# A hybrid encoder layer on one core: a fourth pair of k-tiles as seven products, and work moved between VectorE and ScalarE

## The chip, the cores and the metric

The kernel runs on one core of one Trainium2 chip. The core has five engines that each run their own list of instructions in order and wait for each other by semaphores: TensorE (PE: matrix products; PEld is its loading of the stationary operand), VectorE (DVE), ScalarE (ACT), GpSimd (POOL) and SyncE (SP), which issues most of the DMAs. The metric is the time of one execution in microseconds. The kernel before takes 1113.62 us, the median of three runs from 1113.46 to 1114.1.

## The reference

The layer maps x (256 tokens x 2048, float32) through a norm, one wide input projection, two groups of heads, an output projection and a gate. Cut to what matters:

```python
proj = rmsnorm(x, norm_w) @ w_in            # 2048 x 9*2048
q, v, f_fwd, f_bwd, z_a, b_gate, c_gate, h_b, z_b = split(proj)
# group A, 16 heads of 128, forward and backward:
f = lb + (1 - lb) * sigmoid(f_logit); k = 1 - f
o_a = chunked_linear_recurrence(silu(q), k, v, log(f))       # chunks of 64
o_a = head_rmsnorm(o_a) * silu(z_a)
# group B, 16 groups of 128:
o_b = rmsnorm(b_gate * conv3(c_gate * h_b)) * silu(z_b)
h = x + concat(o_a, o_b) @ w_out
h = h + (p @ w_ple) * sigmoid(h @ w_ple_gate)
out = rmsnorm(h, final_norm_w)
```

## The kernel before

**Products.** Every float32 operand is split into a high and a low part (fp32r), and a product is the sum of high by high, high by low and low by high. The weights come from DRAM through `Stream` (`ws`): a DMA on SP into one of three `raw` tiles, then by halves ("parts") a cast on ScalarE (L121) and a subtraction on VectorE (L122) into one of five `spl` tiles. `get` splits three parts ahead of the part that is used.

**Input projections.** `gemm_in` computes two heads' columns in 16 k-tiles. A k-tile has four products: for each of two accumulators a long one of 512 columns (L428) and a short one of 256 (L426), in the order of `PLAIN`, or of another table where `orders` names one for that k-tile: ONE turns k-tile 1, BOTH turns 1 and 5, TURNED turns 1. `tick()` behind each k-tile counts time in the program, and `at(dt, fn)` puts a function dt ticks later. The order on each engine is that of the framework's scheduler, which looks at priorities and its own estimate of when things are ready; `keep_in_program_order` pins an instruction.

**Group A.** `two_pairs(i)` for i = 0, 2, 4, 6 runs two stages (i, e), e = 0 and 1. A stage has the three projections FF, FB and Q (forget gates forward and backward, and q), each evacuated by a copy of `r` on ScalarE (L488) and an addition on VectorE (L489). `mix_forgets` then makes log f (L624, ScalarE) and 1-f (L628, VectorE), `mix_pair` the scans, exponentials and, on POOL, `kc`, `qc` and `kx`; `scores` the products L736, the masked copies L784 and the product `cx` (L780); `outputs` the product `o` (L799), its squares (L803, ScalarE) and its copy to `ogz` (L804, VectorE). `rest` is issued behind the next pair's first stage: `finish_two` takes the root of the squares' sums (L643, ScalarE) and multiplies `ogz` by root and gate (L649, VectorE), `turn` transposes the result on PE (L659), 32 ticks on, where Q of the next pair's second stage begins: in (2,1), (4,1) and (6,1).

**v and z_a.** For i = 0 they are two separate products (`gemm_two`); for i = 2, 4, 6 `gemm_vz(i)` (here vz2, vz4, vz6) takes both at once, as eight pairs of k-tiles. A pair is 24 products of 512 columns, or, for the pairs in `VZ_SUMS`, seven blocks of three, which is 21 (`half`, L548 to L550), with sums of x (`xsums`, made once, on VectorE at L533, L536 and L544) and sums of weight blocks. The weight sums of a pair in `VZ_OWN` are added on VectorE from the loaded tiles (L83). Those of another pair are prepared in a DRAM tile: `prepare` copies four blocks there from SP (L330), `add_up` adds others in three steps by POOL's accumulating DMAs, and `get` loads them as any weight. Before, VZ_OWN holds all the pairs of VZ_SUMS, and the tiles in DRAM serve the output projection only.

**Order of the stages.** Three first projections fed by DMA (manual order), (0,1), `gemm_two` for V and ZA, then (2,0), (2,1), vz2, (4,0), (4,1), vz4, (6,0), (6,1), vz6; group B with 32 projections of the same form; the output projection; gate and p; the tail.

Of the kernel before, what the change touches and what calls it, by code (L numbers as in the profile page):

```python
# [17 lines left out]
P = 128  # L18
# [119 lines left out]
def tile_hymba_encoder(  # L138
# [26 lines left out]
    xp = xctx.enter_context(tc.tile_pool(name="xp", bufs=1, side="left"))  # L165
# [5 lines left out]
    ws = Stream(tc, rawp, splp, 3)  # L171


    VZ_ORDER, VZ_SUMS, VZ_OWN = range(8), (2, 4, 6), (2, 4, 6)
    dramp = ctx.enter_context(tc.tile_pool(name="dramp", bufs=1, space=bass.MemoryType.DRAM))
    vz_prepared = {}
    blocks = {}
# [57 lines left out]
    rx, rb, rf, most, dummy = (few[:, 2 * j : 2 * j + 2] for j in range(5))  # L235
# [21 lines left out]
    cvw, th = vec[:, 3:6, :], vec[:, 6:10, :].rearrange("p (d j) c -> p d j c", d=2)  # L257


    wz = const.tile([P, P], F32, name="wz")  # L260
    dve.memset(wz, 0.0)

    act.activation(dummy[:, 0:1], wz[:, 0:1], AF.Copy)
# [6 lines left out]
    ident = const.tile([P, P], F32, name="ident")  # L270
# [1 line left out]
    ones = const.tile([P, 1], F32, name="ones")  # L272
    pool.memset(ones, 1.0)

    early = const.tile([P, 2048], F32, name="early")
    smask = early[:, 0:T]
    pool.memset(smask, 1.0)
    pool.memset(smask.rearrange("p (c t) -> p c t", t=CH)[:, :, 0:1], 0.0)
# [3 lines left out]
    for j in range(4):  # L282
        sgn = 1 if j < 2 else -1
        pool.affine_select(
            out=tri[:, j, :], in_=tri[:, j, :], compare_op=ALU.is_ge, fill=0.0, base=0,
# [9 lines left out]
        dve.memset(t, 0.0)  # L295


    mx = const.tile([P, 2, 16], F32, name="mx")
    et = const.tile([P, 2, 2, 16], F32, name="et")
    esum = const.tile([P, 2, 16], F32, name="esum")  # L300
    lb = const.tile([P, 2, 16], F32, name="lb")
    oml = const.tile([P, 2, 16], F32, name="oml")
    noml = const.tile([P, 2, 16], F32, name="noml")
# [60 lines left out]
    xs = xsp.tile([P, NKT, 2, T], F32R, name="xs")  # L364
# [8 lines left out]
    rbc = const.tile([P, T], F32, name="rbc")  # L373
    rbc2 = early[:, T : 2 * T]
    ss8 = const.tile([P, 2, 4], F32, name="ss8")
    rw = [const.tile([P, P], F32, name=f"rw{m}") for m in range(2)]

    def load_tokens(m):
        nc.sync.dma_start(xf32[:, 8 * m : 8 * m + 8].rearrange("p k t -> p (k t)"), xtok[:, m])
# [12 lines left out]
    def x_norms():  # L392
        dve.tensor_reduce(out=rx, in_=ss8, op=ALU.add, axis=AX.X)
        act.activation(rx, rx, AF.Sqrt, bias=epst, scale=1.0 / D)
        dve.reciprocal(out=rx, in_=rx)
        for m in range(2):
            dve.tensor_copy(rw[m], rx[:, m : m + 1].broadcast_to([P, P]))

    def norms_spread():
        rps = psm.tile([P, 512], F32, tag="y", name="rps")  # L400
        for m in range(2):
            pe.matmul(rps[:, m * P : (m + 1) * P], lhsT=rw[m], rhs=ident, start=True, stop=True)
        dve.tensor_copy(rbc, rps[:, :T])  # L403
        dve.tensor_tensor(out=rbc2, in0=rbc, in1=rbc, op=ALU.mult)

# [8 lines left out]
    ONE = {1: SHORTS}  # L414
# [112 lines left out]
    at(14, norms_spread)  # L527


    def act_sums(src, a, s):  # L530


        dve.tensor_tensor(out=a, in0=src[:, :, 0], in1=src[:, :, 1], op=ALU.add)  # L533
        a11, a21, a12, a22 = (a[:, k, m * P : (m + 1) * P] for k in range(2) for m in range(2))
        for o, x, y in ((0, a21, a22), (1, a21, a11), (2, a11, s[:, 0]), (3, a12, s[:, 2])):
            dve.tensor_tensor(out=s[:, o], in0=x, in1=y, op=ALU.subtract)  # L536
# [74 lines left out]
    def mix_forgets(i, xf, qt):  # L611

        by_norms(xf.rearrange("p a b t -> p (a b) t"), rbc, 4)
        by_norms(qt, rbc, 2)
        act.activation(xf, xf, AF.Sigmoid)
        sg = ap_.tile([P, 2, T], F32, tag="sg", name=f"sq{i}")
        act.activation(sg, qt, AF.Sigmoid)
        pool.tensor_tensor(out=qt, in0=qt, in1=sg, op=ALU.mult)

        lf = ap_.tile([P, 2, 2, T], F32, tag="lf", name=f"lf{i}")  # L620
        for d in range(2):
            for h in range(2):
                hd = 2 * i + h
                act.activation(  # L624
                    lf[:, d, h, :], xf[:, d, h, :], AF.Ln,
                    bias=lb[:, d, hd : hd + 1], scale=oml[:, d, hd : hd + 1],
                )
                dve.tensor_scalar(  # L628
                    xf[:, d, h, :], xf[:, d, h, :], noml[:, d, hd : hd + 1], oml[:, d, hd : hd + 1],
                    op0=ALU.mult, op1=ALU.add,  # L630
                )
        return lf

# [34 lines left out]
    def mix_pair(i, xf, qt, lf, here=False):  # L668
# [121 lines left out]
        def outputs(vt, ogz, ss):  # L790

            s, sx = st
            o = psm.tile([P, 2, 2, P], F32, tag="y", name=f"o{i}")
            for h in range(2):
                c = (2 * (i % 2) + h) * P
                hs = slice(c, c + P)
                for m in range(2):
                    pe.matmul(o[:, m, h, :], lhsT=s[:, h, m, :], rhs=vt[:, m, hs], start=True, stop=False)
                    pe.matmul(o[:, m, h, :], lhsT=sx[:, h, 1 - m, :], rhs=vt[:, 1 - m, hs], start=False, stop=True)  # L799
            junk = ap_.tile([P, P], F32, tag="jk", name=f"jk{i}")  # L800
            for h in range(2):
                for m in range(2):
                    act.activation(junk, o[:, m, h, :], AF.Square, accum_out=ss[:, m, h : h + 1])  # L803
            dve.tensor_copy(ogz, o)  # L804

        return scores, outputs

# [5 lines left out]
    def two_pairs(i):  # L813
# [18 lines left out]
        if i == 2:  # L832

            def xsums(z):
                k = 2 * VZ_SUMS[z]
                a, t = xq[1][:, 0].rearrange("p (k t) -> p k t", k=2), xq[1][:, 1].rearrange("p (o t) -> p o t", o=4)
                act_sums(xs[:, k : k + 2], a, t)
                act_split(xq[0][:, z], xs[:, k : k + 2], t)

            for z in range(len(VZ_SUMS)):  # L840
                at(10 + 12 * z, lambda z=z: xsums(z))
        for e in range(2):
            xf = ap_.tile([P, 2, 2, T], F32, tag="xf", name=f"xf{i + e}", bufs=2)
            qt = ap_.tile([P, 2, T], F32, tag="qt", name=f"qt{i + e}")
            first3 = i + e == 0

            kicks = {(0, 1): ({}, ONE, BOTH), (2, 0): (ONE, BOTH, {}), (2, 1): ({}, {}, {})}
            kicks |= {(4, 0): (ONE, TURNED, BOTH), (6, 0): (ONE, TURNED, BOTH)}
            kick = kicks.get((i, e), ({}, {}, BOTH if i + e else {}))
            for j, (c, dst) in enumerate(((B_FF, xf[:, 0]), (B_FB, xf[:, 1]), (B_Q, qt))):  # L850

                acc, offset = acc3[j] if first3 else gemm_in(c, i + e, kick[j]), 500 if e and j == 2 else 200
                evac(acc, lambda m, dst=dst: dst[:, m, :], ap_, offset)

            def mix(e=e, xf=xf, qt=qt):
# [413 lines left out]
```

## Time and profile before

| | |
|---|---|
| median of 3 runs | 1113.62 us |
| profiled execution | 1113.2 us, of it span 1111.2 us |
| around the span | 2.0 us |
| mean granted TensorE clock | 0.998 |
| stages on PE, starts | V and ZA end at 128.2; (2,1) 161.5; vz2 195.7; (4,0) 239.6; (4,1) 278.9; vz4 313.2; (6,0) 357.1; (6,1) 396.4; vz6 430.7; group B 474.6 to 835.6 us |

How to read it: a row of the timeline has start, duration, engine, line, operation and tiles (out <- in), and in brackets how long the engine stood idle before and for whom. Matrix products overlap, so the distance of two starts is what one costs, not its duration. A group has count, busy time and mean duration in ns. A window lists the busy time of PE, PEld, DVE, ACT and POOL in a stretch.

### The profile page before, as it was taken

To read this page: it belongs to the slowest core of one execution; us is meant where nothing else is said; L and a number is where in the kernel's file an instruction comes from. 1 tells how busy PE (TensorE), PEld (TensorE's weight loads), DVE (VectorE), ACT (ScalarE), POOL (GpSimd) and SP (SyncE) were. 2 spreads that over 40 slices of the span, in tenths; PEclk is the share of its full clock that TensorE was granted. 3 is DMA by queue.
4 is the path that set the end of the run, shared out by engine and by line. 5 is a ranking of instruction groups with operands and counts; after the bars stand their busy time and mean duration, and the time that the engine had idled before them with its cause. 6 is when DMAs were issued, how large, how long until landed. Compare 5 with 4: busy or idle time off the path is not lost.

```text
span 1111.2 us, 16886 instructions
## 1 busy us (share of the span) xinstructions
PE 1100.2 (99%) x6455; PEld 947.7 (85%) x6455; DVE 854.4 (77%) x1127; ACT 675.4 (61%) x946; POOL 267.1 (24%) x215
## 2 busy tenths in 40 slices
PE   9999999999999999999999999999999999999997
PEld 8888888888888888888888888888888888888886
DVE  7899468996889778998657848856767888877673
ACT  7787567767876697675535534534546575575562
POOL 1035116103430325043333223424331000000101
PEclk9999999999999999999999999999999999999999
DMA  9755555474447844658999998999979987887542
GB/s 349 271 166 172 183 190 169 135 265 152 159 147 263 305 152 152 224 171 234 299 305 262 255 340 222 289 328 264 290 202 297 326 297 286 288 312 251 196 133 76
DMA packets 69808, 260.44 MB, mean 234 GB/s; under 512 B 7008, under 2 KB 16608, under 8 KB 52192
## 3 DMA queue, kind: packets, MB, share of 16 engines
q1 hardware_dynamic: 60480, 242.25, 62.1%
q0 software_dynamic: 8960, 16.78, 9.8%
q8 instruction: 51, 0.84, 0.3%
q10 hardware_dynamic: 288, 0.34, 0.1%
q14 instruction: 29, 0.24, 0.1%
HBM read 257.25 MB, written 35.65 MB: 264 GB/s over the span
## 4 chain that ended last, share of the span: by engine, by line
PE 93%; DVE 3%; POOL 1%; issue 1%; ACT 1%; DMA 0%; DVEq 0%; ACTq 0%
PE a L428 36%; PE a L426 18%; PE avz L548 3%; PE avz L549 3%; PE avz L550 3%; PE pg L1030 3%; PE pg L1031 3%; PE pg L1029 3%; PE pa L548 2%; PE pa L550 2%; PE pa L549 2%; DVE spl L122 1%; PE pb_sc L550 1%; PE pb_sc L548 1%; PE pb_sc L549 1%; PE cx L780 1%
## 5 line engine op out<-in xcount | busy, mean ns | idle before, releaser
L122 DVE TENSOR_TENSOR spl<-raw,spl 128x1024 fp32r<-128x1024 f32 (+2 forms) x419 | 505.1, 1222 | 165.4 <-ACT spl L121 158.2
L428 PE MATMUL a<-xs,spl 128*128 128x512 f32 x1792 | 621.9, 393 | 0.6 <-DVE xs L368 0.6
L121 ACT CAST spl<-raw 128x1024 fp32r<-128x1024 f32 (+2 forms) x419 | 413.0, 999 | 250.3 <-PE a L426 96.4
L426 PE MATMUL a<-xs,spl 128*128 128x256 f32 x1792 | 494.8, 279 | 0.0
L428 PEld LDWEIGHTS a<-xs,spl 128*128 128x128 f32 x1792 | 334.0, 187 | 74.0 <-ACT spl L121 0.7
L426 PEld LDWEIGHTS a<-xs,spl 128*128 128x128 f32 x1792 | 337.1, 189 | 2.9 <-DVE spl L122 0.3
L1146 POOL TENSOR_TENSOR hh<-hh,fw 128x512 f32<-128x512 f32 (+1 forms) x9 | 10.9, 1225 | 250.7 <-ACT gt L1145 248.0
L488 ACT COPY r<-a 128x256 f32<-128x256 f32 x112 | 40.4, 368 | 34.6 <-PE a L426 33.0
L548 PE MATMUL avz<-spl,xs 128*128 128x512 f32 x138 | 54.0, 391 | 0.0
L550 PE MATMUL avz<-spl,xs 128*128 128x512 f32 x138 | 53.7, 389 | 0.0
L549 PE MATMUL avz<-spl,xs 128*128 128x512 f32 x138 | 53.7, 389 | 0.0
L717 POOL TENSOR_TENSOR qc<-pf,ge 128x256 f32<-128x256 f32 x16 | 22.0, 1379 | 106.7 <-ACT dd L707 89.1
L1029 PE MATMUL pg<-spl,ht 128*128 128x512 f32 (+1 forms) x120 | 45.2, 377 | 0.0
L1030 PE MATMUL pg<-spl,ht 128*128 128x512 f32 (+1 forms) x120 | 45.0, 375 | 0.0
L1031 PE MATMUL pg<-spl,ht 128*128 128x512 f32 (+1 forms) x120 | 45.0, 375 | 0.0
L493 POOL TENSOR_TENSOR xf<-xf,rbc 128x1024 f32<-128x1024 f32 x8 | 20.8, 2603 | 96.9 <-DVE rbc L403 49.5
L121 ACT CAST spl<-early 128x1024 fp32r<-128x1024 f32 (+1 forms) x29 | 28.7, 990 | 19.6 <-PE pb_y L550 7.5
L122 DVE TENSOR_TENSOR spl<-early,spl 128x1024 fp32r<-128x1024 f32 (+1 forms) x29 | 32.8, 1147 | 8.3 <-ACT spl L121 7.8
L548 PE MATMUL pa<-spl,mixa 128*128 128x512 f32 x88 | 34.5, 392 | 0.0
L550 PE MATMUL pa<-spl,mixa 128*128 128x512 f32 x88 | 34.3, 390 | 0.0
L549 PE MATMUL pa<-spl,mixa 128*128 128x512 f32 x88 | 34.3, 389 | 0.0
L946 POOL TENSOR_TENSOR cg<-cg,hb 128x512 f32<-128x512 f32 x8 | 13.7, 1718 | 79.2 <-DVE hb L489 79.2
(321 smaller groups left out, 1650.5 us busy)
## 6 DMA issues: line engine op xcount, KB each, us to landing
raw<-in_w_in_dram SPq DMA_DIRECT2D x106, 1024.0 KB, 7.0
raw<-in_w_in_dram SPq DMA_DIRECT2D x100, 256.0 KB, 3.9
raw<-in_w_out_dram SPq DMA_DIRECT2D x36, 512.0 KB, 5.6
sums<-in_w_out_dram SPq DMA_DIRECT2D x32, 512.0 KB, 10.4
raw<-in_w_in_dram SPq DMA_DIRECT2D x26, 512.0 KB, 5.5
raw<-sums SPq DMA_DIRECT2D x13, 1024.0 KB, 5.2
raw<-in_w_gate_dram SPq DMA_DIRECT2D x9, 1024.0 KB, 4.9
sums<-in_w_out_dram POOLq DMA_DIRECT2D x16, 512.0 KB, 10.5
```

Of the source, the lines that this page charges most:

```text
L121: self.nc.scalar.copy(out=v[:, :, 0], in_=r)
L122: self.nc.vector.tensor_tensor(out=v[:, :, 1], in0=r, in1=v[:, :, 0], op=ALU.subtract)
L426: pe.matmul(a[:, :T], lhsT=lhsT, rhs=xs[:, kt, 0, :], start=False, stop=(kt == NKT - 1))
L428: pe.matmul(a, lhsT=lhsT, rhs=xs[:, kt, :, :].rearrange("p s n -> p (s n)"), start=(kt == 0), stop=False)
L488: act.copy(out=r, in_=acc[m][:, 1, :])
L548: pe.matmul(acc, lhsT=ah, rhs=w[:, 0], start=start, stop=False)
L549: pe.matmul(acc, lhsT=ah, rhs=w[:, 1], start=False, stop=False)
L550: pe.matmul(acc, lhsT=al, rhs=w[:, 0], start=False, stop=stop)
L717: pool.tensor_tensor(out=c64(dst[:, d]), in0=c64(src[:, d, :, half * P : (half + 1) * P]), in1=g.unsqueeze(3).broadcast_to([P, 2, 2, CH]), ...
L1029: pe.matmul(acc[m], lhsT=lh, rhs=wh, start=(kt == 0), stop=False)
L1030: pe.matmul(acc[m], lhsT=lh, rhs=wl, start=False, stop=False)
L1031: pe.matmul(acc[m], lhsT=ll, rhs=wh, start=False, stop=(kt == nk - 1))
```

## The change

A pair more is taken as seven products, pair 5, with its weight sums in DRAM. 1-f goes from VectorE to an Identity activation on ScalarE (32 instructions), and the copy of `o` to `ogz` goes from VectorE to ScalarE (8). The first addition of each of x's sums is pinned to its place in the program. Three tables of product orders change. Some small tiles move to other pools, so that the larger `xsum` fits.

```diff
-    VZ_ORDER, VZ_SUMS, VZ_OWN = range(8), (2, 4, 6), (2, 4, 6)
+    VZ_ORDER, VZ_SUMS, VZ_OWN = range(8), (2, 4, 5, 6), (2, 4, 6)
...
-    rw = [const.tile([P, P], F32, name=f"rw{m}") for m in range(2)]
...
+        rw.append(ap_.tile([P, 2, P], F32, tag="s", name="rw"))
...
-    def act_sums(src, a, s):
-        dve.tensor_tensor(out=a, in0=src[:, :, 0], in1=src[:, :, 1], op=ALU.add)
+    def act_sums(src, a, s, place=lambda instr: instr):
+        place(dve.tensor_tensor(out=a, in0=src[:, :, 0], in1=src[:, :, 1], op=ALU.add))
...
-                dve.tensor_scalar(
-                    xf[:, d, h, :], xf[:, d, h, :], noml[:, d, hd : hd + 1], oml[:, d, hd : hd + 1],
-                    op0=ALU.mult, op1=ALU.add,
+                act.activation(
+                    xf[:, d, h, :], xf[:, d, h, :], AF.Identity,
+                    bias=oml[:, d, hd : hd + 1], scale=noml[:, d, hd : hd + 1],
                 )
...
-            dve.tensor_copy(ogz, o)
+            act.copy(out=ogz, in_=o)
...
-                act_sums(xs[:, k : k + 2], a, t)
+                act_sums(xs[:, k : k + 2], a, t, tc.keep_in_program_order)
...
-            kicks = {(0, 1): ({}, ONE, BOTH), (2, 0): (ONE, BOTH, {}), (2, 1): ({}, {}, {})}
-            kicks |= {(4, 0): (ONE, TURNED, BOTH), (6, 0): (ONE, TURNED, BOTH)}
+            kicks = {(0, 1): ({}, {k: SHORTS for k in (1, 5, 9)}, BOTH), (2, 0): (ONE, BOTH, {}), (2, 1): ({}, {}, {})}
+            kicks |= {(i, e): ((ONE, TURNED, BOTH), ({}, {}, {}))[e] for i in (4, 6) for e in range(2)}
```

`kick.get` gave Q of (4,1) and (6,1) the table BOTH before; now it is empty. From L400 on the new code's lines stand two further down (L643 is now L645, L659 is L661).

The scheduler orders the engines anew. **ScalarE in (4,1)**, from the last square (L803) of the pair before on, as it was:

```order
L803 ACTIVATE jk_2714,ss_1332<-o_2705 128x128
L121 CAST spl_2811<-raw_2809 128x4x256
L488 COPY r<-a_4_1_2631 128x256
L706 ACT_TABLE_LOAD
L706 ACTIVATE pf_2755<-dd_2756 128x512
L643 ACT_TABLE_LOAD
L643 ACTIVATE ss_1332<-ss_1332,epst 128x8
L121 CAST spl_2830<-raw_2809 128x4x256
```

The root of `ss` stood one cast (L121) behind the last square. Now, on the same engine and in the same stage, the stretch that ends with it (`spl_2932`, `spl_2961` and `spl_2982` are the first three parts of Q's weights, `a_5_0` FF's and FB's accumulators):

```order
L121 CAST spl_2932<-raw_2930 128x4x256
L490 COPY r<-a_5_0_2816 128x256
L490 COPY r<-a_5_1_2817 128x256
L121 CAST spl_2961<-raw_2930 128x4x256
L709 ACT_TABLE_LOAD
L709 ACTIVATE dd_2784<-dd_2784 128x512
L121 CAST spl_2982<-raw_2980 128x4x256
L645 ACT_TABLE_LOAD
L645 ACTIVATE ss_1341<-ss_1341,epst 128x8
L121 CAST spl_3027<-raw_2980 128x4x256
```

The root now stands six casts behind the last square. From the first of the four squares to it stand on ScalarE, apart from seven casts, one L630, a load and an activation for `ge`, two evacuation copies, two `pf`, two `dd`, the copy of `ogz`, and the gates `sq` and two `sz` with their loads.

**PE where Q of (4,1) begins**, before and now (`ogt` are the transposes of the two heads' `ogz`, `a_5_0` and `a_5_1` the accumulators of Q):

```order
L659 MATMUL ogt_2968<-ident,ogz_2447 128x128 x4
L659 MATMUL ogt_2977<-ident,ogz_2704 128x128 x4
L428 MATMUL a_5_0_2992<-xs,spl_2899 128x512
L426 MATMUL a_5_0_2992<-xs,spl_2899 128x256
L428 MATMUL a_5_1_2993<-xs,spl_2899 128x512
```

```order
L661 MATMUL ogt_3001<-ident,ogz_2474 128x128 x4
L661 MATMUL ogt_3010<-ident,ogz_2732 128x128
L430 MATMUL a_5_0_3025<-xs,spl_2932 128x512
L428 MATMUL a_5_0_3025<-xs,spl_2932 128x256
L430 MATMUL a_5_1_3026<-xs,spl_2932 128x512
L661 MATMUL ogt_3010<-ident,ogz_2732 128x128 x3
L428 MATMUL a_5_1_3026<-xs,spl_2932 128x256
```

Three of Q's products stand between the fifth transpose and the last three. On VectorE, the order behind the new root is the reciprocal, four L651, the split of `spl_3027`, two L651, the first half of FB's evacuation, two L651. (6,1) has the same orders on all three engines.

**VectorE ahead of the second scores of the pair i = 0** (L784, in the new code L786, behind the gate logarithms), before and now, from the end of Q's evacuation in (0,1) on:

```order
L489 TENSOR_TENSOR qt_518<-a_1_1_783,r 128x256
L122 TENSOR_TENSOR spl_907<-raw_904,spl_907 128x2x512
L708 TENSOR_TENSOR dd_654<-xf_497,dd_654 128x512
L122 TENSOR_TENSOR spl_922<-raw_904,spl_922 128x2x512
L628 TENSOR_SCALAR xf_517<-xf_517,noml,oml 128x256 x2
L122 TENSOR_TENSOR spl_940<-raw_937,spl_940 128x2x512
L628 TENSOR_SCALAR xf_517<-xf_517,noml,oml 128x256
L122 TENSOR_TENSOR spl_955<-raw_937,spl_955 128x2x512
L628 TENSOR_SCALAR xf_517<-xf_517,noml,oml 128x256
L544 TENSOR_TENSOR xsum<-xd,xsum 128x4x128
L122 TENSOR_TENSOR spl_1056<-raw_1053,spl_1056 128x2x512
L784 COPY_PREDICATED early<-early,scps_164 128x512
```

```order
L491 TENSOR_TENSOR qt_518<-a_1_1_784,r 128x256
L122 TENSOR_TENSOR spl_912<-raw_909,spl_912 128x2x512
L122 TENSOR_TENSOR spl_927<-raw_909,spl_927 128x2x512
L122 TENSOR_TENSOR spl_945<-raw_942,spl_945 128x2x512
L122 TENSOR_TENSOR spl_960<-raw_942,spl_960 128x2x512
L122 TENSOR_TENSOR spl_1061<-raw_1058,spl_1061 128x2x512
L786 COPY_PREDICATED early<-early,scps_166 128x512
```

The instructions of 1-f have left VectorE. x's sums, of which three stood before these copies (three L533, twelve L536, three L544), now all stand in (2,0), behind both masked copies of this pair.

More of the change, by code (lines that the diff above doesn't have):

```diff
@@ L257, in tile_hymba_encoder @@
     cvw, th = vec[:, 3:6, :], vec[:, 6:10, :].rearrange("p (d j) c -> p d j c", d=2)
-    wz = const.tile([P, P], F32, name="wz")
+    early = const.tile([P, 2048], F32, name="early")
+    wz = early[:, 1024 : 1024 + P]
     dve.memset(wz, 0.0)
@@ L273, in tile_hymba_encoder @@
     pool.memset(ones, 1.0)
-    early = const.tile([P, 2048], F32, name="early")
     smask = early[:, 0:T]
@@ L295, in tile_hymba_encoder @@
         dve.memset(t, 0.0)
-    mx = const.tile([P, 2, 16], F32, name="mx")
-    et = const.tile([P, 2, 2, 16], F32, name="et")
-    esum = const.tile([P, 2, 16], F32, name="esum")
+    mx = xp.tile([P, 2, 16], F32, name="mx")
+    et = xp.tile([P, 2, 2, 16], F32, name="et")
+    esum = xp.tile([P, 2, 16], F32, name="esum")
     lb = const.tile([P, 2, 16], F32, name="lb")
@@ L395, in x_norms @@
         dve.reciprocal(out=rx, in_=rx)
+        rw.append(ap_.tile([P, 2, P], F32, tag="s", name="rw"))
         for m in range(2):
-            dve.tensor_copy(rw[m], rx[:, m : m + 1].broadcast_to([P, P]))
+            dve.tensor_copy(rw[0][:, m], rx[:, m : m + 1].broadcast_to([P, P]))
+    rw = []
     def norms_spread():
@@ L401, in norms_spread @@
         for m in range(2):
-            pe.matmul(rps[:, m * P : (m + 1) * P], lhsT=rw[m], rhs=ident, start=True, stop=True)
+            pe.matmul(rps[:, m * P : (m + 1) * P], lhsT=rw[0][:, m], rhs=ident, start=True, stop=True)
         dve.tensor_copy(rbc, rps[:, :T])
```

## The prediction

> **What bounds the kernel now.** I read the page's totals and slices first, then the chain, then the list of what TensorE (PE) waited for.
>
> ```profile
> span 1111.2 us, 16886 instructions
> ...
> PE 1100.2 (99%) x6455; PEld 947.7 (85%) x6455; DVE 854.4 (77%) x1127; ACT 675.4 (61%) x946; POOL 267.1 (24%) x215
> ...
> PEclk9999999999999999999999999999999999999999
> ...
> PE 93%; DVE 3%; POOL 1%; issue 1%; ACT 1%; DMA 0%; DVEq 0%; ACTq 0%
> ```
>
> ```profile
> engine line waited for: us in total, times, longest us
> PE wps L266 <- DVE wz L261: 1.1, 1, 1.1
> PE cx L780 <- POOL kx L723: 1.1, 1, 1.1
> PE a L428 <- DVE xs L368: 0.6, 1, 0.6
> ```
>
> PE is busy for 99% of the span, at full clock in every slice, and the chain runs through it. It has one wait in the body, 1.1 us before `cx`. So the time moves in three ways only: columns that PE no longer streams, the pace at which products follow each other, and new holes in PE's stream. I price these three against the profiled run: its span of 1111.2 us and 2.0 us around it are 1113.2 us, 0.4 under the median of 1113.62. About 0.2%, or 2.23 us, is what a measurement of this kernel can tell from no change.
>
> **The products.** Three `gemm_vz` calls each turn a pair of 24 products into one of 21, so nine products of 512 columns go.
>
> ```profile
> 201.01 0.39 PE L549 MATMUL avz<-spl,xs 128*128 128x512 f32 x1
> ...
> 205.79 0.39 PE L549 MATMUL avz<-spl,xs 128*128 128x512 f32 x1
> ```
>
> The 21 steps between these two starts take 4.78 us, 0.2276 each (the 0.39 us of a row overlap the next). Nine are **-2.05 us**, and PE has nothing to put in their place.
>
> **The wait before cx.** The chain behind the one body wait runs through a DVE that is full: 49.30 of 50 us in the window that precedes it.
>
> ```profile
> core 0: us, PE busy (x) PEld busy (x) DVE busy (x) ACT busy (x) POOL busy (x), PEclk, DMA share, GB/s
> ...
> 50.00:100.00 50.00, 50.00 (x333) 42.52 (x333) 49.30 (x71) 38.26 (x51) 19.46 (x13) 1.00 0.52 169
> ```
>
> ```profile
> 94.19 1.37 DVE L784 COPY_PREDICATED early<-early,scps 128x512 f32<-128x512 uint32 x2
> ...
> 104.10 0.68 DVE L708 TENSOR_TENSOR dd<-xf,dd 128x512 f32<-128x512 f32 x1
> ```
>
> ```profile
> 103.05 3.35 POOL L717 TENSOR_TENSOR kc<-dd,ge 128x256 f32<-128x256 f32 x1 [6.22 <-DVE pf L709]
> ...
> 111.16 1.91 POOL L723 TENSOR_TENSOR kx<-kc,ge 128x512 f32<-128x512 f32 x1
> ```
>
> DVE reaches the masked copies L784 at 94.19, then the scans and L708/L709; POOL starts at 103.05 and hands over `kx` at 113.07. The change takes out of DVE's order ahead of L784 the eight L628, and of the three early sums three L533, twelve L536 and three L544, as the third pair of lists above shows.
>
> ```profile
> L628 DVE TENSOR_SCALAR xf<-xf,noml,oml 128x256 f32<-128x256 f32 x32 | 13.9, 442 | 4.6 <-ACT lf L624 4.6
> ...
> L536 DVE TENSOR_TENSOR xd<-xd 128x128 f32<-128x128 f32 x12 | 4.0, 370 | 0.2
> ...
> L533 DVE TENSOR_TENSOR xd<-xs 128x512 f32<-128x512 f32 x3 | 2.1, 688 | 0.1
> ...
> L544 DVE TENSOR_TENSOR xsum<-xd,xsum 128x512 fp32r<-128x512 f32 x3 | 2.0, 681 | 0.0
> ```
>
> That is 8 x 0.44 + 2.1 + 4.0 + 2.0 = 11.6 us of work. A tenth of it moving the chain is enough, and the tick that issues the scores is late next. I take the whole wait: **-1.1 us**. The bound on the other side is 0, if `kx` stays where it is.
>
> The four sums now stand in the stage (2,0). Their 4 x 2.7 us (11.6 - 3.5 us is three of them) and one more split lie there on a DVE with room: 30.20 us busy in 100 to 150 us by the same table of windows, with PE working on products that need only the splits. I cost them at nothing; without that cover they would hold a split back by about one sum, 2.7 us.
>
> ```profile
> 100.00:150.00 50.00, 48.94 (x340) 42.27 (x339) 30.20 (x32) 28.61 (x48) 11.36 (x7) 1.00 0.56 190
> ```
>
> **Other product orders.** In-projections run at two paces. A long and a short product in a fast one take 11.09 us for 32 pairs, as FF of (4,1) does from 278.85 to 289.94; a slow one takes about 0.2 us more.
>
> ```profile
> 278.85 0.39 PE L428 MATMUL a<-xs,spl 128*128 128x512 f32 x1
> ...
> 289.94 0.39 PE L428 MATMUL a<-xs,spl 128*128 128x512 f32 x1
> ...
> 301.04 1.03 PE L659 MATMUL ogt<-ident,ogz 128*128 128x128 f32 x8
> 301.83 0.48 PE L428 MATMUL a<-xs,spl 128*128 128x512 f32 x1
> ...
> 313.18 0.40 PE L548 MATMUL avz<-spl,xs 128*128 128x512 f32 x1
> ```
>
> ```profile
> 184.49 0.48 PE L428 MATMUL a<-xs,spl 128*128 128x512 f32 x1
> ...
> 195.68 0.39 PE L548 MATMUL avz<-spl,xs 128*128 128x512 f32 x1
> ```
>
> Q of (4,1), after its eight transposes and with BOTH, takes 313.18 - 301.83 = 11.35 us. Q of (2,1), after the same transposes with no turned order, takes 11.19. The change takes BOTH from Q of (4,1) and (6,1): 2 x -0.16 = **-0.3 us**. FB of (0,1) gets three turned k-tiles for one. Slow with one, it may stay so (0) or turn fast (-0.2, with its Q -0.4); its nearest row is its own, so 0.
>
> **The seven-product pair itself.** Pair 5 now brings seven blocks of 512 to split where a plain pair has four, in 21 steps of 0.2276 = 4.78 us. Then pair 6 has its own sums added on DVE.
>
> ```profile
> L83 DVE TENSOR_TENSOR raw<-raw 128x1024 f32<-128x1024 f32 x9 | 14.3, 1588 | 0.0
> ...
> L83 DVE TENSOR_TENSOR raw<-raw 128x512 f32<-128x512 f32 x18 | 13.7, 762 | 0.6
> ```
>
> DVE needs 3.5 x 1.13 us for pair 5's splits and 1.59 + 2 x 0.76 = 3.1 us for the sums: 7.1 us against 9.56 us of PE in the two pairs, plus pair 6's own 3.5 x 1.13 = 4.0. That is 11.1 us: DVE falls 1.5 us behind, and `Stream` splits three parts ahead, two to three of 1.13 us at that point, 2.3 to 3.4 us. I take 0.1 us for each call, **+0.3 us**, between 0 and 0.9 (the shortfall, if the lead is half gone). The sums in DRAM come by POOL's queue in three steps; the page has these transfers for w_out:
>
> ```profile
> sums<-in_w_out_dram POOLq DMA_DIRECT2D x16, 512.0 KB, 10.5
> ```
>
> POOL has 11.36 us of work in the whole of 100 to 150 us. Three steps of 10.5 us from 114 us, when `kx` and its followers are out, are done by 146; vz2 starts at 195.68 and asks later still. Hidden; late, they would cost up to a transfer of 10.5 us a call.
>
> **The head norm before the turn.** The cost that I find is on ScalarE. The 1-f of eight instructions a pair and two copies of `ogz` now stand in its order ahead of the square root `ss`, and the order shown above for (4,1) has that root after the cast of the third Q part, where before it stood one cast behind the squares.
>
> ```profile
> 277.65 0.28 ACT L803 ACTIVATE jk<-o 128x128 f32<-128x128 f32 x1 [0.88 <-PE o L799]
> ...
> 282.66 1.28 ACT L643 ACT_TABLE_LOAD   x1
> 283.95 0.30 ACT L643 ACTIVATE ss<-ss,epst 128x8 f32<-128x8 f32 x1
> 284.16 1.04 ACT L121 CAST spl<-raw 128x1024 fp32r<-128x1024 f32 x1
> ...
> 300.89 0.37 ACT L488 COPY r<-a 128x256 f32<-128x256 f32 x1
> 301.23 1.05 ACT L121 CAST spl<-raw 128x1024 fp32r<-128x1024 f32 x1
> ```
>
> ```profile
> 291.57 1.48 DVE L649 SCALAR_TENSOR_TENSOR ogz<-ogz,ss,zt 128x128 f32<-128x128 f32 x4 [1.20 <-POOL zt L639]
> ...
> 297.74 0.60 DVE L649 SCALAR_TENSOR_TENSOR ogz<-ogz,ss,zt 128x128 f32<-128x128 f32 x2
> ```
>
> Before, the root is done at 284.2, the last L649 at 298.3, and the transposes run at 301.04 without a gap: 2.7 us to spare. From 277.65 ScalarE has hardly an idle moment, so its new order can be added up from the steps between starts in these rows (cast 0.95, load 1.28, 512-wide function 0.55, square 0.40, copy of `r` 0.30). Three L630 ahead of the squares cost 1.5 us less the 0.88 idle, so they begin at 278.2. Up to the root stand 4 squares (1.6), one L630 (0.5), 6 loads (7.7), 7 casts (6.65), 7 functions (3.85), 4 copies (1.2), the copy of `ogz` (0.55), `ge` and the root (0.4): 22.45 us, root done at 300.7. The same count made on the old rows up to 301.23 gives 300.8, so I add 0.4: 301.1. Then DVE has the reciprocal (0.15), four L651 (1.5), a split (1.13), two L651 (0.6), an evacuation (0.36) and two L651 (0.6): the last `ogz` at 305.4. PE has only three products to put between. They free 0.5 us, so Q goes on at 305.4 - 0.5 for 301.83, **+3.1 us**. Behind the waiting transposes on PE stands all of Q, and behind PE everything. (6,1) has the same order, its first square at 395.15 for 277.65. Two such waits are 6.2; I take **+6.0**. The bounds are +0.4, if ScalarE is so early that only the order of the split and the evacuation holds (0.2 each), and +8, with each step 0.06 us longer.
>
> The load of the root's table is 1.28 us in the row, and the root starts at once behind it. The Trainium skill, in "ScalarE: Activation LUTs", section "What ACT_TABLE_LOAD costs", puts a switch at 1283 ns for the load and some 1380 ns more for a drain. By that, the six loads would put the root 8.3 us later each time and the sum at an estimated +19 us; the trace (282.66 to 283.95) shows no drain, and the row decides.
>
> **Sum:** -2.05 - 1.1 - 0.3 + 0.3 + 6.0 = +2.85 us; 1113.2 + 2.85 = 1116.05, and 0.4 for the median: **1116.4 us**.
>
> **Rivals.**
> 1. *The head norm is in time*, and the case ends on the other side. It holds if ScalarE reaches the root by about 298, where its casts only wait for PE; for it speaks the 2.7 us to spare before, against it the count. Then +0.4 for +6.0: 1113.62 - 2.05 - 1.1 - 0.3 + 0.3 + 0.4 = **1110.9 us**. All else is -3.15 us, so it decides by what the two waits come to: under 0.9 us is faster, up to 5.4 us is no change, more is slower.
> 2. *The granted clock falls in the wait.* PEclk is 9 in every slice of the page, also over the 1.1 us wait at 112, so no row shows it for 3 us. If products ran at half rate for as long as each wait, 3.1 us, it would add 2 x 1.55: **1119.5 us**. The Trainium skill ("TensorE: Matmul & The Clock Gate", "What's actually happening") has the clock halved after an idle window of about 3.4 us, which these waits would just miss; no run here shows it yet.
> 3. *Group B turns slow.* After `gemm_vz` the first projection now has its first two k-tiles in another order. If the 32 projections of group B took the 0.16 us that Q lost, 5.1 us: **1121.5 us**. Against it: FF of (4,1), three projections behind a `gemm_vz`, is fast in the rows above.
> 4. *The change does less than it says:* the wait at `cx` stays or the sums in DRAM come late, 1.1 to 5 us on top: **1117.5 to 1121 us**. POOL is idle when the sums are due, which speaks against it.
>
> **How the numbers follow.** Forecast (the two waits cost 4 to 7 us in all) 0.57, rival 1 0.30, rival 2 0.05, rival 3 0.03, rival 4 0.05. The forecast's own range, 1114.5 to 1117.5, crosses the bound of 1115.85, and I count three quarters of its chance as slower, 0.43; with two thirds of rivals 2 to 4, **slower 0.52**. Rival 1 gives faster 0.22 and same 0.08; **faster 0.23, same 0.25** with the rest. The range takes in rival 1 and rival 2: **1110.4 to 1119.6**.
>
> **What would show it.** Right: two idle stretches on PE of 2 to 4 us ahead of L661 in (4,1) and (6,1), released by DVE's `ogz`; none ahead of `cx`; pairs 5 of `avz` 4.8 us long with no hole in pair 6. If the transposes run without a gap, the count of ScalarE's order was wrong and rival 1 holds. If PEclk falls behind them, rival 2. If the products of group B are further apart than 11.1 us for a projection, rival 3.

## The result and the profile after

The changed kernel takes 1133.22 us, the median of six runs (1125.55 to 1134.18), against 1113.54 us of the kernel before. Five of the six lie between 1132.56 and 1134.18; the run of 1125.55 left no profile, so why it was shorter is open. The ratio is 1.0166, with a 95% interval of 1.0139 to 1.0193. The forecast of "slower" held; its 1116.4 us and its upper end of 1119.6 did not. The profiled execution has a span of 1130.8 us, 19.6 more than before.

The totals of the page, and its chain:

```profile
span 1130.8 us, 16946 instructions
...
PE 1111.3 (98%) x6446; PEld 949.0 (84%) x6446; DVE 841.7 (74%) x1099; ACT 707.2 (63%) x997; POOL 273.5 (24%) x227
...
PE 79%; ACT 8%; DVE 5%; POOL 3%; DMA 2%; issue 2%; SPq 0%; DVEq 0%; ACTq 0%; POOLq 0%
```

PE has nine instructions fewer and is busy 11.1 us longer, so much of the loss is no wait: products of the same form run slower. The chain leaves PE for a fifth of the span, where it was 93% before. The list of what PE waited for:

```profile
PE scps L738 <- POOL qc L719: 4.1, 1, 4.1
PE ogt L661 <- DVE ogz L651: 3.4, 6, 1.1
PE ey L551 <- DVE spl L122: 1.2, 2, 0.9
PE wps L267 <- DVE early L262: 1.1, 1, 1.1
PE pa L551 <- DVE spl L122: 0.8, 1, 0.8
PE pa L550 <- ACT spl L121: 0.5, 1, 0.5
```

The wait for `kx` ahead of `cx` is gone. The forecast waits of L661 are there. The largest of the list, 4.1 us ahead of scores, was in no step of the prediction.

The starts of products on PE's timeline, cut at the borders of the stages, give the whole account (us; before, then the differences from it, one profile each; e2, e3, e15 and e16 are experiments described below):

| stretch of PE's timeline | before | after | e2 | e3 | e15 | e16 |
|---|---|---|---|---|---|---|
| start to the end of Q of (0,1) | 75.10 | -0.39 | 0.00 | +2.33 | +0.76 | +0.95 |
| V and ZA | 53.09 | -1.15 | -1.15 | -1.15 | -1.19 | -1.19 |
| Q of (2,1) | 11.18 | +0.21 | +0.21 | +0.21 | 0.00 | 0.00 |
| vz2, vz4, vz6 | 131.67 | +0.24 | +0.10 | 0.00 | +0.10 | +3.10 |
| FF, FB and turn of (4,1) and (6,1) | 45.96 | +5.00 | +4.96 | +4.97 | +4.99 | +2.28 |
| Q of (4,1) and (6,1) | 22.70 | +1.11 | +2.61 | +0.91 | +2.47 | -0.16 |
| (2,0), rest of (2,1), (4,0), (6,0) | 134.87 | +0.35 | +0.16 | +0.03 | +0.09 | +0.21 |
| group B, first three projections | 39.28 | +5.93 | +0.19 | +0.01 | +5.83 | +0.08 |
| group B, the other 29 | 321.72 | +6.16 | +6.16 | +6.16 | +6.16 | 0.00 |
| output projection | 166.39 | +1.86 | -0.02 | +1.19 | +1.15 | +1.10 |
| gate and p, to the last product | 100.75 | +0.03 | 0.00 | 0.00 | +0.03 | +0.03 |

Three stretches hold 17 of the 19.6 us. **The pace of group B** is the first. On PE's timeline of the changed kernel, two neighbouring projections start at

```profile
536.45 0.40 PE L430 MATMUL a<-xs,spl 128*128 128x512 f32 x1
...
547.75 0.40 PE L430 MATMUL a<-xs,spl 128*128 128x512 f32 x1
```

11.30 us apart. In the kernel before, two neighbours of the same stage, one projection further on, start at 536.03 and 547.13, 11.10 apart:

```profile
536.03 0.39 PE L428 MATMUL a<-xs,spl 128*128 128x512 f32 x1
...
547.13 0.39 PE L428 MATMUL a<-xs,spl 128*128 128x512 f32 x1
```

Between them PE waits for nothing, the list of products is the same, and the granted clock is 1.00 in both; 29 of them make 6.16 us. **The first scores of group B** are the second. The timeline of POOL after, and then before:

```profile
498.63 1.54 POOL L719 TENSOR_TENSOR qc<-pf,ge 128x256 f32<-128x256 f32 x1 [7.51 <-ACT ge L706]
500.14 1.75 POOL L495 TENSOR_TENSOR cg<-cg,early 128x512 f32<-128x512 f32 x1
501.84 1.03 POOL L338 DMA_DIRECT2D sums<-in_w_out_dram  x1
502.45 2.74 POOL L719 TENSOR_TENSOR kc<-dd,ge 128x256 f32<-128x256 f32 x2
505.26 1.39 POOL L725 TENSOR_TENSOR kx<-kc,ge 128x512 f32<-128x512 f32 x1
506.61 1.59 POOL L719 TENSOR_TENSOR qc<-pf,ge 128x256 f32<-128x256 f32 x1
```

```profile
489.47 0.62 POOL L717 TENSOR_TENSOR qc<-pf,ge 128x256 f32<-128x256 f32 x1 [5.83 <-DVE pf L709]
490.72 1.00 POOL L717 TENSOR_TENSOR kc<-dd,ge 128x256 f32<-128x256 f32 x1 [0.63 <-DVE dd L708]
491.69 1.60 POOL L717 TENSOR_TENSOR qc<-pf,ge 128x256 f32<-128x256 f32 x1
```

Before, the second `qc` was done at 493.3, and the scores began behind the second projection of group B, which started at 487.47. After, that projection starts 5.4 us later (492.89), and the second `qc` is done 14.9 us later, at 508.2: it stands last, behind `cg`, a DMA issue, both `kc` and `kx`, and the chain to it is itself later (ScalarE gives `ge` at 498.55). PE's timeline and the windows around the wait:

```profile
503.88 0.28 PE L428 MATMUL a<-xs,spl 128*128 128x256 f32 x1
508.26 0.42 PE L738 MATMUL scps<-qc,dd 128*32 128x128 f32 x2 [4.09 <-POOL qc L719]
```

```profile
core 0: us, PE busy (x) PEld busy (x) DVE busy (x) ACT busy (x) POOL busy (x), PEclk, DMA share, GB/s
500.00:503.00 3.00, 3.00 (x20) 2.63 (x19) 3.00 (x4) 2.26 (x3) 3.00 (x4) 1.00 0.78 246
...
508.20:510.40 2.20, 2.14 (x80) 2.14 (x80) 0.70 (x2) 0.00 (x0) 0.00 (x1) 0.51 0.76 198
510.40:512.00 1.60, 1.60 (x20) 1.54 (x12) 1.60 (x4) 0.00 (x0) 1.47 (x1) 0.61 0.91 379
512.00:516.00 4.00, 4.00 (x25) 3.54 (x25) 3.10 (x5) 1.50 (x2) 3.16 (x4) 1.00 0.22 21
...
301.00:304.00 3.00, 1.31 (x8) 0.71 (x7) 3.00 (x8) 2.34 (x5) 1.17 (x2) 1.00 0.81 206
```

Behind the wait the granted clock is 0.51 and 0.61 in these two windows, and full again from 512 on; that is the part of the 5.9 us which is no wait. **The turn** is the third:

```profile
301.59 0.33 PE L661 MATMUL ogt<-ident,ogz 128*128 128x128 f32 x1 [0.42 <-DVE ogz L651]
302.12 0.59 PE L661 MATMUL ogt<-ident,ogz 128*128 128x128 f32 x3 [0.20 <-DVE ogz L651]
303.77 0.33 PE L661 MATMUL ogt<-ident,ogz 128*128 128x128 f32 x1 [1.06 <-DVE ogz L651]
303.88 0.47 PE L430 MATMUL a<-xs,spl 128*128 128x512 f32 x1
304.18 0.28 PE L428 MATMUL a<-xs,spl 128*128 128x256 f32 x1
304.30 0.39 PE L430 MATMUL a<-xs,spl 128*128 128x512 f32 x1
304.63 0.59 PE L661 MATMUL ogt<-ident,ogz 128*128 128x128 f32 x3
```

```profile
300.23 0.30 ACT L645 ACTIVATE ss<-ss,epst 128x8 f32<-128x8 f32 x1
```

The root is done at 300.5, where the count gave 301.1. The waits of the one turn add up to 1.7 us, those of both to the 3.4 of the list; the rest of the +5.00 is the slow pace of FF and FB, 0.84, and transposes that no longer run together.

### The profile page after: what moved, and what is told of

It is laid out like the page before. It is cut to its first block, busy times and chain, and to the rows that moved or that the text cites. A ratio compares the mean times of both kernels' runs of the same rounds, so it can differ in the third digit from the quotient of the medians.

```text
span 1130.8 us, 16946 instructions
## 1 busy us (share of the span) xinstructions
PE 1111.3 (98%) x6446; PEld 949.0 (84%) x6446; DVE 841.7 (74%) x1099; ACT 707.2 (63%) x997; POOL 273.5 (24%) x227
## 4 chain that ended last, share of the span: by engine, by line
PE 79%; ACT 8%; DVE 5%; POOL 3%; DMA 2%; issue 2%; SPq 0%; DVEq 0%; ACTq 0%; POOLq 0%
PE a L430 29%; PE a L428 15%; ACT spl L121 3%; PE pg L1032 3%; PE pg L1031 3%; PE pg L1033 3%; DVE spl L122 2%; PE avz L550 2%; PE avz L552 2%; PE avz L551 2%; PE pa L551 1%; PE pa L552 1%; PE pa L550 1%; PE a L449 1%; DMA raw<-in_w_in_dram 1%
## 5 line engine op out<-in xcount | busy, mean ns | idle before, releaser
L430 PE MATMUL a<-xs,spl 128*128 128x512 f32 x1792 | 629.4, 398 | 0.0
L121 ACT CAST spl<-raw 128x1024 fp32r<-128x1024 f32 (+2 forms) x425 | 419.2, 996 | 244.3 <-PE a L428 94.8
L550 PE MATMUL avz<-spl,xs 128*128 128x512 f32 x120 | 47.0, 392 | 0.0
L551 PE MATMUL avz<-spl,xs 128*128 128x512 f32 x120 | 46.7, 389 | 0.0
L552 PE MATMUL avz<-spl,xs 128*128 128x512 f32 x120 | 46.7, 389 | 0.0
L121 ACT CAST spl<-early 128x1024 fp32r<-128x1024 f32 (+1 forms) x29 | 28.6, 990 | 18.5 <-PE pb_y L552 7.5
```

What stands on the lines that cost most here:

```text
L121: self.nc.scalar.copy(out=v[:, :, 0], in_=r)
L430: pe.matmul(a, lhsT=lhsT, rhs=xs[:, kt, :, :].rearrange("p s n -> p (s n)"), start=(kt == 0), stop=False)
L550: pe.matmul(acc, lhsT=ah, rhs=w[:, 0], start=start, stop=False)
L551: pe.matmul(acc, lhsT=ah, rhs=w[:, 1], start=False, stop=False)
L552: pe.matmul(acc, lhsT=al, rhs=w[:, 0], start=False, stop=stop)
```

## The experiments

(Kicks are the tables of product orders.) Theory A was that the waits of the new orders explain all, the slow pace being what the long wait leaves behind; theory B that the pace has a cause of its own, in the orders of products.

**e1_root: the root raised in priority.**

```diff
+        with tc.high_priority(offset=400):
             act.activation(ss, ss, AF.Sqrt, bias=epst, scale=1.0 / P)
             dve.reciprocal(out=ss, in_=ss)
```

> The changed kernel with finish_two's root and reciprocal raised in priority, which puts the root right behind the last square, as before. Theory (the turn waits come from ScalarE's order alone): PE runs the eight transposes in (4,1) and (6,1) without a gap, 2 x 2.3 us go, and all else stays: about 1128.5 us. Rival (VectorE's splits and the gate's products on POOL are late as well): the waits shrink to 1 us or less each, 1130 to 1132 us.

1131.42 us (1127.06 to 1134.68). FF, FB and turn lose their wait (5.00 over before falls to 0.84, which is the slow pace), and Q is as fast as forecast. But vz4 is now 6.01 us longer than before and vz6 1.82, where they had been -0.07 and -0.46. Part of vz4's loss is the clock: it is granted at 0.50 from 351.65 to 358.48 us. ScalarE in vz4 of this run:

```profile
340.11 2.00 ACT L121 CAST spl<-raw 128x1024 fp32r<-128x1024 f32 x2 [0.72 <-DMA raw<-vz]
343.30 1.05 ACT L121 CAST spl<-raw 128x1024 fp32r<-128x1024 f32 x1 [1.19 <-DMA raw<-in_w_in_dram]
347.60 0.62 ACT L121 CAST spl<-raw 128x512 fp32r<-128x512 f32 x1 [3.25 <-DMA raw<-in_w_in_dram]
```

The casts wait for loads. The moved data of this run's DMA from 320 to 350 us, in 40 slices:

```profile
GB/s 318 288 322 208 12 22 0 0 0 0 0 0 0 0 5 206 288 294 251 157 273 306 273 197 120 76 0 193 305 290 287 240 224 281 255 314 370 412 453 407
```

For some 7 us, from 323 to 330.5, next to nothing is loaded. I read this as the three raw tiles being held: the pair with its sums in DRAM takes two of them (the blocks, and the sums) where a plain pair or one with its own sums takes one. That reading was not tried by itself. By it, the turn waits had given the loads time to catch up, and without them the time was paid in the next stage (e11, below, speaks against that as the whole story).

**e2_scores_first: the last pair's chain, from the gate exponents to kx, raised in priority.**

```diff
+        with tc.high_priority(offset=200) if here and i == 7 else ExitStack():
             ...
             pool.tensor_tensor(out=kx, in0=kc, ...)
```

> The changed kernel with the last pair's chain from the exponents to kx raised in priority (POOL then has qc, kc, qc, kc, kx ahead of cg's product and its DMA). Theory A (the slow pace of group B follows from the 4.3 us wait at its first scores): the wait goes (-4.3 to -5.7) and the 28 projections behind it run at 11.09 us instead of 11.31 (-6.1): about 1121.5 us. Theory B (the slow pace comes from the order of the products behind gemm_vz, or from the kicks): only the wait goes, about 1128 us, projections of 11.31.

1127.12 us (1126.25 to 1127.88). The wait is gone, 5.7 us with the clock behind it. The pace is not: 6.16 us, to the hundredth. Theory A falls as the only cause of the pace.

The same profile shows something else. The turn of (4,1) has the waits that the changed kernel has to within 0.01 us, 0.41, 0.20 and 1.07, but here the clock is halved behind them, and Q of (4,1) takes 2.06 us more than before instead of 0.55:

```profile
core 0: us, PE busy (x) PEld busy (x) DVE busy (x) ACT busy (x) POOL busy (x), PEclk, DMA share, GB/s
301.80:305.20 3.40, 1.95 (x10) 1.21 (x10) 3.40 (x11) 1.92 (x5) 0.76 (x1) 1.00 0.81 181
305.25:308.66 3.41, 3.41 (x13) 2.99 (x12) 3.11 (x6) 1.34 (x3) 1.88 (x1) 0.50 0.87 264
308.70:312.00 3.30, 3.30 (x20) 2.85 (x19) 1.23 (x1) 2.57 (x3) 0.46 (x1) 1.00 0.12 41
```

e8 and e15 have it too, in the same place. Why the same waits cost the clock in these runs and not in the changed kernel's profile was not tried.

**e3_no_pair: three pairs as seven products again.**

```diff
-    VZ_ORDER, VZ_SUMS, VZ_OWN = range(8), (2, 4, 5, 6), (2, 4, 6)
+    VZ_ORDER, VZ_SUMS, VZ_OWN = range(8), (2, 4, 6), (2, 4, 6)
```

> The changed kernel with three pairs as seven products again, as before; 1-f and the ogz copies stay on ScalarE, the kicks stay new. Theory: the turn waits stay (2 x 2.3 us), the wait at group B's first scores goes with POOL's old order, vz2's waits of 1.2 us go, nine products come back (+2.05). With theory A group B is fast: 1133.2 - 5.8 - 6.1 - 1.2 + 2.05 = about 1122 us; with theory B slow: about 1128 us.

1125.91 us (1124.28 to 1127.52). The scores' wait is the pair's: it goes with it, and the stages of `gemm_vz` are at 0.00. Turn waits and pace stay, so the fourth pair causes neither. (Its +2.33 at the start, in the table, goes with a wait of 1.7 us there and a granted clock of 0.50 for 3.41 us behind it.)

**e4_root_and_scores: both repairs.**

> Both repairs of the changed kernel together: root and the last pair's chain raised in priority. Theory A: 1133.2 - 4.6 - 5.7 - 6.1 = about 1117 us; theory B: about 1123 us.

1126.86 us (1125.30 to 1128.35). Scores' and turn waits are gone and the pace stays, as theory B has it; the time is 4 us over its sum, and the three `gemm_vz` take 7.0 us more than before.

Between what stays in all four (layout, kicks, 1-f and ogz, pinned sums) four more kernels decide.

**e5_layout_alone: the kernel before with the small tiles moved.**

```diff
-    wz = const.tile([P, P], F32, name="wz")
+    early = const.tile([P, 2048], F32, name="early")
+    wz = early[:, 1024 : 1024 + P]
...
-    mx = const.tile([P, 2, 16], F32, name="mx")
+    mx = xp.tile([P, 2, 16], F32, name="mx")
...
+        rw.append(ap_.tile([P, 2, P], F32, tag="s", name="rw"))
```

> The kernel before with the small tiles moved as in the changed one (early first, mx, et, esum in xp, rw in ap) and nothing else. Theory M (where the tiles lie in memory sets the slow pace): Q of (2,1) at 11.4 us and the 28 later projections of group B at 11.31, +6.4 us: about 1120.5 us. Rival (kicks or the work moved to ScalarE set it): no change, 1114 us.

1120.93 us (1120.59 to 1122.04), ratio 1.0040 (1.0025 to 1.0056) to a kernel before that ran at 1116.08 on that chip. In its profile the 29 projections are +6.16 us, and FF and FB of (4,1) and (6,1) are slow as well, +0.21 each; all else is within 0.4. The order of products is unchanged. So the place of tiles sets the pace, though Q of (2,1), of which I expected the same, stayed fast.

**e6_kicks_alone: the kernel before with the new product orders.**

> The kernel before with the new tables of product orders alone. Theory M: group B at 11.09, as before; FB and Q of (0,1) become fast (-0.3), Q of (4,1) and (6,1) -0.16 each: about 1113.4 us. Rival K (the new kicks at (0,1) leave a phase behind that group B inherits): Q of (2,1) and group B slow, about 1120 us.

1117.13 us (1113.42 to 1118.86), ratio 0.9997 (0.9983 to 1.0012): no change. Q of (4,1) and (6,1) are 0.17 faster each, as expected; but in e5, which has the old orders, they are 0.14 faster too, so this does not show that the orders did it. Group B starts at 11.09; in the profile one projection takes 11.62 us in the middle, and all behind it 11.31. Such a jump in mid-stage shows that the pace can tip in a kernel of the old layout too.

**e7_scalar_alone: the kernel before with 1-f and the ogz copies on ScalarE.**

> The kernel before with 1-f and the ogz copies on ScalarE alone. Theory: the turn waits of 2 x 2.3 to 2.5 us come with it, the 1.1 us before cx go partly (1-f has left VectorE, the sums have not): 1114 + 4.6 - 0.6 = about 1118 us, group B at 11.09. Rival (the move sets the slow pace as well): about 1124 us.

1121.27 us (1120.92 to 1123.81), ratio 1.0047. The turn's stretch is +2.51 twice, V and ZA -0.85 (so 1-f alone shortens the wait at `cx` to 0.3 us), and group B tips in mid-stage as in e6 (one projection of 12.58, then 11.31). In the projection in which it tips, PE stands idle for 0.76 us for a split on VectorE and, 3 us later, for another 0.15 us; the pace is fast between the two and slow behind the second.

**e8_no_pair_old_layout: e3 with the small tiles at their old places.**

> The changed kernel with three pairs as seven products (as in e3_no_pair) and with the small tiles where they lay before; kicks, 1-f, ogz and pinned sums stay new. Theory M: group B at 11.09, Q of (2,1) at 11.19, so e3_no_pair's time less 6.4: about 1119.5 us. Rival (not the layout): as e3_no_pair, 1126 us.

1121.30 us (1118.05 to 1123.41). In the profile the 29 projections are +0.00: with the old layout, and all else of e3, the pace is fast. The turn stays at +2.52 twice.

Which of the moved tiles does it? The weights' raw and spl tiles, xs, `ident`, `early`, and the tiles of the pool ap have all moved.

**e9_xs_back and e10_half_shift: e5 with empty bytes ahead of xs, and ahead of raw, spl and xs.**

```diff
+    xsp.tile([P, 512], F32, name="pad")        # e9
+    const.tile([P, 256], F32, name="pad")      # e10
```

> e5_layout_alone with 2048 bytes of nothing ahead of xs, so that xs lies where it lay before (byte 95168 of a partition) and the weights' raw and spl tiles where the changed kernel has them (2048 lower). If the place of xs sets the pace: group B at 11.09 us a projection, 28 projections -6.2 us against e5, about 1114.5 us. If the place of spl or of the small tiles sets it: 11.31, about 1120.9 us.

> e5_layout_alone with 1024 bytes of nothing ahead of raw, spl and xs, so that all three lie 1024 lower than before instead of 2048. If only a step of 2048 bytes or a certain place matters, group B is at one of the two paces without saying which; I expect 11.09 (a kernel's own place is slow in few cases), 1114.5 us, against 11.31 and 1121 us if any shift from the old place makes it slow.

1120.74 and 1120.79 us, one run each; +6.16 in both profiles. So the place of xs does not set the pace, nor does it matter whether raw, spl and xs lie 1024 or 2048 bytes lower, and what I expected of e10 was wrong.

**e11_ogz_back: the changed kernel with the ogz copies on VectorE.**

```diff
-            act.copy(out=ogz, in_=o)
+            dve.tensor_copy(ogz, o)
```

> The changed kernel with the copies of ogz back on VectorE; the root then stands five casts behind the last square instead of six, and PE's list has the eight transposes together again. Theory (the ogz copies make most of the turn waits): 2 x 2.1 to 2.5 us go, and vz4 and vz6 get waits of 1 to 5 us in their place, as in e1_root: between 1128 and 1132 us. Rival (1-f does): the turn waits stay at 2 us or more each, about 1133 us. Group B stays at 11.31.

1126.89 us (1126.40 to 1130.46). The turn's wait shrinks from 3.4 to 0.4 us in all, and the two stretches from +5.00 to +2.16, of which 0.84 is pace. vz2 is +1.74, vz4 and vz6 are at -0.18 and -0.38: the price that e1 paid did not come due here, so it hangs on more than the missing wait. Why is open.

**e12_sums_and_kicks: the kernel before with the sums of x pinned, and the new product orders.**

> The kernel before with two parts of the change alone: x's sums pinned to their place, and the new product orders. Layout, 1-f, ogz and the pairs stay as before. The wait of 1.1 us at cx goes, FB and Q of (0,1) become fast (-0.3), Q of (4,1) and (6,1) -0.17 each: -1.7 us, about 0.2% faster than before. If the sums cost as much in (2,0) as they free earlier: no change.

1114.51 us (1111.92 to 1117.12, twelve runs), ratio 1.0002 (0.9991 to 1.0014): no change that can be measured, on a chip where the runs of before spread from 1112.32 to 1116.55. Its profile has V and ZA at -1.19 and no wait at `cx`, so the sums take that wait away (the orders alone, in e6, leave it at 1.1 us). Q of (4,1) and (6,1) did not get faster this time (+0.04).

**e13_rw_move_alone and e14_rw_other_tag.** In the pool ap a tag's place is set by who asks first. With `rw` as the first tile of the tag s, `s` comes first and the attention tiles behind it lie 2048 bytes higher.

```diff
-        rw.append(ap_.tile([P, 2, P], F32, tag="s", name="rw"))
+        rw.append(ap_.tile([P, 2, P], F32, tag="sg", name="rw"))   # e14, on e5's kernel
```

> The kernel before with rw alone moved into the pool ap under the tag s, as the change does. That puts s first in that pool, and sq, lf, pf, dd, kc, qc and kx 2048 bytes higher. Theory A (the places of these attention tiles, which PE reads between the projections, set the pace it falls into): group B at 11.31 us a projection, about 1121 us. Theory C (early, ident and the small constants set it): 11.09, about 1114.5 us.

> e5_layout_alone with rw under the tag sg instead of s. All of the attention tiles then lie where they lay before; early, ident, the constants, raw, spl and xs lie as in the changed kernel. Theory A: group B at 11.09, about 1114.5 us. Theory C: 11.31, about 1121 us.

1120.12 and 1114.21 us, one run each. e13 runs its projections at 11.31 from the fourth to all but the last four (+5.76 in all), e14 all at 11.09 (+0.00). The same two projections of e5 and then of e14, which is e5 with one word changed:

```profile
525.99 0.40 PE L430 MATMUL a<-xs,spl 128*128 128x512 f32 x1
...
537.29 0.40 PE L430 MATMUL a<-xs,spl 128*128 128x512 f32 x1
```

```profile
525.96 0.39 PE L430 MATMUL a<-xs,spl 128*128 128x512 f32 x1
...
537.05 0.39 PE L430 MATMUL a<-xs,spl 128*128 128x512 f32 x1
```

So it is the places of the attention tiles, and not those of raw, spl, xs, `ident` or `early`, which e14 has where the changed kernel has them. One run each could be chance, since the pace can tip, but FF of (4,1) decides the same way in every profile of this case: it takes 11.31 us in all ten kernels with `rw` first under the tag s, and 11.09 in all eight with the attention tiles at their old places.

**e15_all_but_rw: the changed kernel with that one word.**

> The changed kernel with rw under the tag sg, nothing else. Theory A: Q of (2,1) back at 11.19 and the 28 later projections of group B at 11.09, -6.2 us: about 1127 us; turn waits and the wait at group B's scores stay. Theory C: as the changed kernel, about 1133 us.

1133.59 us. Q of (2,1) is back (0.00), but group B is still at +6.16. Theory A as written fails here: with the long wait at the scores in place, the pace is slow even with the old places. FF of (4,1) and of (6,1) are fast in this run, and group B is slow only from behind the wait on.

**e16_repaired: that word, e2's priority, e11's copies.**

> The changed kernel without the three faults found: rw under the tag sg, the last pair's chain raised in priority, the copies of ogz on VectorE. Theory A: 1133.2 - 6.2 - 5.9 - 2.9 = about 1118 us, still slower than before by what vz2's waits, the rest of the turn waits and the output projection take; with theory C about 1124 us. If the fourth pair's waits were only those, it would be under 1114.

1116.20 us (1114.09 to 1119.36), ratio 1.0010 (0.9997 to 1.0023): 17 us won back. Group B is at 0.00. In the profiled execution, of 1119.36 us, vz2 alone is +3.67, with two waits (1.2 and 0.9 us) and then 3.41 us at a granted clock of 0.50. What PE waits for now:

```profile
PE a L430 <- ACT spl L121: 1.3, 1, 1.3
PE ogt L661 <- DVE ogz L651: 1.3, 4, 0.6
PE ey L551 <- DVE spl L122: 1.3, 2, 0.9
PE ey L550 <- ACT spl L121: 1.2, 1, 1.2
PE wps L267 <- DVE early L262: 1.1, 1, 1.1
PE pa L551 <- DVE spl L122: 0.8, 1, 0.8
```

The places of the attention tiles are therefore enough for the slow pace (e2, e5, e13). That the wait at the scores is enough as well rests on e15's one run and on e7, where pauses of under 1 us came ahead of the tip; a tip with no wait in the list, as in e6, is not ruled out. With both gone the pace is fast (e16). No version here beats the kernel before by more than the measurement tells.

## Why the prediction was wrong

- *The products*: right in count (6446 of PE's instructions for 6455). Their 2.05 us show only where little was lost: vz4 is at -0.58 in e2 and -0.61 in e15, of the -0.68 that three products are.
- *The wait before cx, -1.1*: right; -1.15. e7 and e12 show that either half of the relief was nearly enough: 1-f alone gives -0.85, the sums alone -1.19.
- *Other product orders, -0.3*: not shown. Q of (4,1) and (6,1) are 0.17 shorter with the new orders alone (e6), but 0.14 shorter with the old ones in e5, and not shorter with the new ones in e12; in the changed kernel they began behind a broken turn and were 0.55 longer each. FB and Q of (0,1), which I had put at 0, are 0.12 and 0.16 shorter; but e7 and e13 have that with the old orders, and e2 and e15 lack it in Q with the new.
- *The seven-product pair itself, +0.3*: mis-sized. The three stages stand at +0.24 with 2.05 us of products gone: 2.3 us lost, 1.2 of it in the list as waits of `ey`, and 9.0 lost in e4, with 5.6 of such waits and half the clock for 3.4 us. I had bounded it by VectorE's work, 0 to 0.9; by e1's rows casts waited for loads.
- *The head norm before the turn, +6.0*: right, in place and sum. The two turns and the Q behind them are +6.1, and +5.8 in e7 without the rest of the change. The idle stretches are shorter than forecast, 1.7 us each for 2 to 4 (2.1 in e7); the rest lies in the slow pace of FF and FB, in the broken-up transposes and in Q. That the sum fits this well is partly luck. The cause is as argued, the order of ScalarE (e1); e11 shows that the copies of `ogz` make most of it.
- *The failed step* is, first, the list of what could open a hole in PE's stream. I followed the scalar engine's new order into (4,1) and (6,1), and took rival 4's "POOL is idle when the sums are due" for all of POOL. I did not follow POOL's order into the start of group B, where POOL now runs the last `qc` behind `kx`: 5.9 us, the pair's own price (e3).
- *The second failed step* is the pace at which products follow each other, one of the three ways in which the time could move. I gave it a term for the product orders alone and none for the small tiles: 6.16 us in group B. With the 5.9 us this is 12.1 of the 16.8 us by which the forecast was short. "Slower" came out, but the turn that it stood on is 6.1 of the 19.6 us.
- *Rival 3* gave group B's slow pace 0.03 and laid it on the order of products. The pace was slow, at 6.16 us instead of 5.1, and the change's line on small tiles was one sufficient cause; the orders alone left group B's start fast (e6).
- *Rival 2*, the clock: in the changed kernel's profile not behind the turn waits, where PEclk stayed 1.00 (301 to 304 us), but behind the 4.1 us wait, 0.51. In e2, e8 and e15 it did come true at the turn of (4,1): half the clock for 3.41 us, and 1.4 to 1.5 us more in Q than in the changed kernel, where I had priced 1.55 a turn. The Trainium skill ("TensorE: Matmul & The Clock Gate", "What's actually happening") has the clock halved after at least one idle window of about 3.4 us; the wait of 4.09 us agrees with that, but in e2 waits of at most 1.07 us were enough, with PE busy for 1.95 of the 3.40 us before, and here the measurement decides.
- *Open*: the up to 1.9 us in the output projection, which e2, e6 and e14 do not have and the others do; why the places of tiles that PE reads between projections set its pace behind them; the raw tiles as the cause in `gemm_vz`; why e1 paid there and e11 did not; and when short waits cost the clock.

## What to carry to other kernels

Where a scheduler orders the engines, a change of one stage is read on every engine and in every later stage in which something waits: the largest wait here came where no changed line stands. A move of tiles in memory is a change like any other, and is tried alone. And on a stream that is 99% busy, measure the distance of products as well as the waits, since a third of the loss had no wait at all. Short waits close together can also cost the clock behind them (e2).

## What the runs showed of the hardware

- A stream of identical products has two paces, 11.09 and 11.31 us for 64 products in the same order at a granted clock of 1.00, and mostly keeps the one it falls into. Which one depends on the places of tiles used between (2048 bytes in the pool ap: +6.16 us in e5 against e14) and, by one run, on a wait ahead of it (e15). It tipped in mid-stage in e6 and e7, with the old places, and back to fast in e13.
- A pause of PE of 4.1 us is followed by a granted clock of 0.5 to 0.6 in the next 3.8 us. Shorter ones can halve it too: behind waits of 0.41, 0.20 and 1.07 us within 3 us the clock was 0.50 for 3.41 us in e2, while behind the same waits it stayed at 1.00 in the changed kernel.
- Taking one wait away can bring others: with the turn waits gone by the root's priority, vz4 and vz6 took 8.4 us more (e1 against the changed kernel), so that little was gained. With most of them gone by the copies of `ogz` they did not (e11).
